# Hybrid retention and RG-LRU layer: five of the eight recurrent input blocks computed by token and turned by DMA, gate matmuls spread one tile a unit

## The chip, the cores and the metric

The kernel runs on one core of one Trainium2 chip. The metric is the time of one execution in device microseconds (us). The kernel before takes 1972.18 us as the median of three runs, which lie between 1972.11 and 1972.3 us.

## The reference, cut to what matters

One decoder layer on 256 tokens of width 2048, everything in float32. The first matrix product, `hn @ w_in`, makes eight slices. Two of them feed the recurrent mixer: `xr` (the recurrent input) and `yr` (its gate).

```python
hn = rmsnorm(h, norm_mix_w[l])
q, k, v, g_ret, xr, yr, g_a, g_b = jnp.split(hn @ w_in[l], offsets, axis=-1)
...                                                     # retention over q, k, v, g_ret -> ret_out
xr = causal_dwconv(xr, rnn_conv_w[l], rnn_conv_b[l])    # 4 taps over the tokens
hr = rg_lru(xr, ...)                                    # 16 blocks of 128 features:
#   gate_r = sigmoid(xb @ w_a + b_a); gate_i = sigmoid(xb @ w_x + b_x)
#   h_t = a_t h_{t-1} + sqrt(1 - a_t^2) (gate_i * xr)_t     a scan over the tokens
rnn_out = jax.nn.gelu(yr) * hr
merged = sigmoid(g_a) * (ret_out @ w_proj_ret[l]) + sigmoid(g_b) * (rnn_out @ w_proj_rnn[l])
h = h + merged @ w_mix_out[l]
...                                                     # cross-attention, conv gated FFN, final norm
```

The convolution and the scan run along the tokens, so the recurrent mixer wants its data with features on the partitions and tokens along the free dimension ("by feature").

## The kernel before

**Products in two parts.** Each float32 matrix is split into a high and a low part (`hi`, `lo` for weights; the two halves of an `s` tile for the activations), and a product is made of three: high by high, activation low by weight high, activation high by weight low. Weights come in pieces of 512 by 512 (1 MB). The work on one piece is a **unit**. A block of 512 output columns of `w_in` takes four units.

**What a unit needs.** `prefetch` issues the DMA of a piece into one of six `raw` buffers on SP's queue, ScalarE (ACT) makes `hi` from it (L288), VectorE (DVE) makes `lo` (L289). Each of `hi` and `lo` has three buffers, and `units` keeps two pieces prepared ahead of the one TensorE (PE) works on. So the cast of a piece can start only when PE has done with the high part of the piece three before it.

**Two ways to multiply.** `gemm_t` leaves its result by feature: the weight is the stationary operand, and the activations move. Per unit it issues 16 matmuls with `hi` that move 512 columns (high and low half of the activations side by side) and 16 with `lo` that move 256 (high half only), and needs two accumulators (`acc`), which are added up afterwards (`joined`: an ACT copy of one half at L552, a DVE addition at L553). `gemm_n` leaves its result by token: the activations are stationary and the weight moves. Per unit it issues 24 matmuls that all move 512 columns, into one accumulator. There are three accumulators in all, of two PSUM banks each.

**Turning by DMA.** A by-token result is turned to by-feature in four steps, which the FFN uses for nearly all of its blocks: `row_planes` splits each float32 word into two 16-bit planes (`rp`), two DMA transposes on SP's queue turn the planes (`d`), `join_planes` puts the words together again (`jp`, four ACT copies a block), and a DVE multiplication by `rsb2` applies the norm's factor of each token.

**The stage that is changed.** `recurrent(b)` for the groups b = 0 to 3 computes two blocks each with `gemm_t`: the recurrent input (`O_XR`, then the convolution into `xr`) and the gate (`O_YR`, then a gelu into `gl`). `recur(b)` follows: `gates(j)` for the four feature tiles (two small matmuls `sm` each at L972, then four ACT functions), then `weigh`, `drive` and `scan`, whose result is stored to DRAM as `rnn`. Group 0 also carries the end of the retention of heads 4 to 7. After the four groups come blocks of `w_in` in pairs.

**What sets the order.** The program is written in units; `later(n, fn)` runs `fn` after n further units. A scheduler then orders each engine's instructions; each engine and each DMA queue runs its own list in order. `tc.keep_in_program_order` holds an instruction at its place in the written order.

Of the kernel before, what the change touches and what calls it, by code (L numbers as in the profile page):

```python
# [14 lines left out]
ALU = mybir.AluOpType  # L15
# [5 lines left out]
NT = D // P  # L21
# [7 lines left out]
BW = 512  # L29
# [12 lines left out]
O_XR, O_YR, O_GA, O_GB = 6144, 8192, 10240, 12288  # L42
# [114 lines left out]
def hybrid_layer(  # L157
# [16 lines left out]
    act, dve, pe, pool, sp = nc.scalar, nc.vector, nc.tensor, nc.gpsimd, nc.sync  # L174
# [17 lines left out]
    def big(shape, dt=F32, s="b"):  # L192
        return bp.tile(shape, dt, tag="big", name=nm(s))
# [112 lines left out]
    def later(n, fn):  # L306

        pending.append((step[0] + n + 1, fn))
# [21 lines left out]
    def gemm_t(w, row, st, nk, col):  # L330

        accs = [acc(), acc()]
        first = gemms[0] == 0
        phase = 0
        for k0, parts in chunks(nk, w, row, col):
            last = k0 + KC >= nk
            tiles = [(kk, j) for j in range(2) for kk in range(KC)]
            if first and k0 == 0:
                runs = [[(t, pr, kk, j) for t in (0, 1)] for pr in range(2) for kk in range(KC) for j in range(2)]
            elif last:  # L340
                runs = [[(t, pr, kk, j) for kk, j in tiles] for pr in range(2) for t in (1 - pr, pr)]
            else:
                runs = [[(t, pr, kk, j) for pr in range(2) for kk, j in tiles] for t in (phase, 1 - phase)]
                phase = 1 - phase
            for i, run in enumerate(runs):
                for t, pr, kk, j in run:
                    k = k0 + kk
                    sx = st[k // 2][:, k % 2, :]
                    part = parts[kk // KH][t][:, kk % KH, (2 * pr + j) * P : (2 * pr + j + 1) * P]
                    a = accs[pr][:, j, :]  # L350
                    if t == 1:
                        a, sx = a[:, S:BW], sx[:, 0:S]
                    pe.matmul(  # L353
                        a, part, sx, start=k == 0 and t == 0, stop=k == nk - 1 and t == 0, skip_group_check=True
                    )
                if i + 1 == len(runs) // 2 and not last:
                    st[(k0 + KC) // 2 + 1]
        return accs
# [14 lines left out]
    def gemm_n(w, row, st, nk, col):  # L373

        a = acc()
        for k0, parts in chunks(nk, w, row, col):
            ops = [
                [halves(st[(k0 + k) // 2], (k0 + k) % 2, slice(tt * P, (tt + 1) * P)) for k in range(KC)]
                for tt in range(2)
            ]  # L380
            for tt in range(2):
                upper_n(a[:, tt, :], ops[tt], parts, k0 == 0)
            for tt in range(2):
                lower_n(a[:, tt, :], ops[tt], parts, k0 + KC >= nk)
        return a
# [272 lines left out]
    xs = Pairs(x_t, p_mix)  # L658
# [21 lines left out]
    rsb2 = rsb[:, None, :].to_broadcast([P, 2, S])  # L680

    def scaled(a, s):
        z = joined(a, s)
        dve.tensor_tensor(out=z, in0=z, in1=rsb2, op=ALU.mult)
        return z
# [72 lines left out]
    def words(t):  # L758

        return t.bitcast(U16).rearrange("p t (w two) -> p t w two", two=2)  # L760

    def planes(t, rows, cs=slice(0, BW)):

        for i in range(2):
            act.copy(t[:, :, i, cs], words(rows)[:, :, :, 1 - i])

    def join_planes(d, pr):

        t = tmp("jp")
        for i in range(2):  # L770
            ins = act.copy(words(t)[:, :, :, 1 - i], d[:, i, 2 * pr : 2 * pr + 2, :])  # L771
            if i == 0:
                tc.keep_in_program_order(ins)
        return t

    def row_planes(o):

        t = big([P, 2, 2, BW], U16, s="rp")
        planes(t, o)
        return t  # L780

    def turn_planes(rows):

        d = big([P, 2, KC, S], U16, s="d")
        for tt in range(2):
            sp.dma_start_transpose(
                out=d.rearrange("p a c s -> p (a c) s")[:, :, tt * P : (tt + 1) * P],
                in_=rows[:, tt].rearrange("p a w -> p (a w)"),
            )
        return d  # L790
# [115 lines left out]
    for g in range(2):  # L906
        dec = big([P, 4, S], s="dec")
        vs, turned = [], []
        for b, o in enumerate((O_Q, O_K)):
            a = qjoin if g == b == 0 else [joined(t, "q") for t in gemm_t("w_in", 0, xs, NT, o + g * BW)]  # L910
# [53 lines left out]
    def recur(b, rgw, xr, gl):  # L964
        aa, tt_, ti = big([P, 4, S], s="aa"), big([P, 4, S], s="tt"), big([P, 4, S], s="ti")

        def gates(j):
            t = 4 * b + j
            c1 = slice(t, t + 1)
            gp = small()  # L970
            for i in range(2):
                pe.matmul(gp[:, i, :], rgw[:, i, j, :], xr[:, j, :], start=True, stop=True)  # L972
            tr = tp.tile([P, S], F32, tag="tr", bufs=2, name=nm("tr"))
            act.activation(tr, gp[:, 0, :], AF.Tanh, scale=0.5, bias=half_ba[:, c1])
            act.activation(ti[:, j, :], gp[:, 1, :], AF.Tanh, scale=0.5, bias=half_bx[:, c1])
            act.activation(aa[:, j, :], tr, AF.Exp, scale=neg_half_c[:, c1], bias=neg_half_c[:, c1])
            act.activation(tt_[:, j, :], tr, AF.Tanh, scale=half_c[:, c1], bias=half_c[:, c1])

        def weigh():
            for pr in range(2):  # L980
                cs = slice(2 * pr, 2 * pr + 2)
                a2 = tmp("a2")
                dve.tensor_tensor(out=a2, in0=aa[:, cs, :], in1=aa[:, cs, :], op=ALU.mult)
                dve.scalar_tensor_tensor(
                    out=tt_[:, cs, :], in0=a2, scalar=1.0, in1=tt_[:, cs, :], op0=ALU.add, op1=ALU.mult
                )
            act.activation(tt_, tt_, AF.Sqrt, scale=0.25)

        def drive():
            dve.scalar_tensor_tensor(out=ti, in0=ti, scalar=1.0, in1=xr, op0=ALU.add, op1=ALU.mult)  # L990
            dve.tensor_tensor(out=ti, in0=ti, in1=tt_, op=ALU.mult)

        def scan():
            for j in range(4):
                dve.tensor_tensor_scan(
                    out=xr[:, j, :], data0=aa[:, j, :], data1=ti[:, j, :], initial=0.0, op0=ALU.mult, op1=ALU.add
                )
            for pr in range(2):
                o = tmp("rn")
                cs = slice(2 * pr, 2 * pr + 2)  # L1000
                dve.tensor_tensor(out=o, in0=xr[:, cs, :], in1=gl[:, cs, :], op=ALU.mult)
                rnn.store(o)

        for j in range(4):
            later(j // 2, lambda j=j: gates(j))
        for n, fn in zip((2, 3, 4) if b < 3 else (6, 11, 17), (weigh, drive, scan)):
            later(n, fn)

    def recurrent(b):
        rgw = big([P, 2, 4, P], s="rgw")  # L1010
        for i, src in enumerate((rg_w_a, rg_w_x)):
            sp.dma_start(out=rgw[:, i], in_=src[0, 4 * b : 4 * b + 4].rearrange("g i j -> i g j"))
        xr = big([P, 4, S], s="xr")
        for pr, a in enumerate(gemm_t("w_in", 0, xs, NT, O_XR + b * BW)):
            z = scaled(a, "xz")
            for j in range(2):
                t = 4 * b + 2 * pr + j
                y = xr[:, 2 * pr + j, :]
                act.activation(y, z[:, j, :], AF.Identity, scale=p_cw(3, t), bias=p_cb(t))
                for s in range(1, 4):  # L1020
                    dve.scalar_tensor_tensor(
                        out=y[:, s:S], in0=z[:, j, 0 : S - s], scalar=p_cw(3 - s, t), in1=y[:, s:S],
                        op0=ALU.mult, op1=ALU.add,
                    )
        gl = big([P, 4, S], s="gl")
        for pr, a in enumerate(gemm_t("w_in", 0, xs, NT, O_YR + b * BW)):
            y = scaled(a, "yz")
            y2, th = tmp("y2"), tmp("yt")
            act.activation(y2, y, AF.Square)
            dve.tensor_scalar(out=y2, in0=y2, scalar1=0.044715 * K0, scalar2=K0, op0=ALU.mult, op1=ALU.add)  # L1030
            dve.tensor_tensor(out=y2, in0=y2, in1=y, op=ALU.mult)
            act.activation(th, y2, AF.Tanh)
            dve.scalar_tensor_tensor(
                out=gl[:, 2 * pr : 2 * pr + 2, :], in0=th, scalar=1.0, in1=y, op0=ALU.add, op1=ALU.mult
            )
        later(0, lambda: recur(b, rgw, xr, gl))

    merged, merged_sums = [], []

# [463 lines left out]
```

## Time and profile before

| | |
|---|---|
| Median of three runs | 1972.18 us |
| The profiled execution, its time | 1972.37 us |
| Its span, first to last instruction | 1970.6 us |
| PE busy | 1959.8 us, 99% of the span |
| DVE, ACT busy | 1563.9 us (79%), 1299.7 us (66%) |
| Mean granted TensorE clock | 0.999 |
| Weight DMAs | 373 of 1 MB, 40 of them on GpSimd's queue |

The page lists busy time per engine, the chain of work that ended last, and groups of instructions by source line. A matmul's listed duration (some 0.39 us) includes its way through the array; matmuls overlap, so the pace is read from the distance between starts. The changed stage lies at about 272 to 482 us of the span.

### The profile page before, as it was taken

To read this page: it belongs to the slowest core of one execution; us is meant where nothing else is said; L and a number is where in the kernel's file an instruction comes from. 1 tells how busy PE (TensorE), PEld (TensorE's weight loads), DVE (VectorE), ACT (ScalarE), POOL (GpSimd) and SP (SyncE) were. 2 spreads that over 40 slices of the span, in tenths; PEclk is the share of its full clock that TensorE was granted. 3 is DMA by queue.
4 is the path that set the end of the run, shared out by engine and by line. 5 is a ranking of instruction groups with operands and counts; after the bars stand their busy time and mean duration, and the time that the engine had idled before them with its cause. 6 is when DMAs were issued, how large, how long until landed. Compare 5 with 4: busy or idle time off the path is not lost.

```text
span 1970.6 us, 23609 instructions
## 1 busy us (share of the span) xinstructions
PE 1959.8 (99%) x9264; PEld 1645.2 (83%) x9264; DVE 1563.9 (79%) x1546; ACT 1299.7 (66%) x1353; POOL 43.2 (2%) x52
## 2 busy tenths in 40 slices
PE   9999999999999999999999999999999999999998
PEld 8888888888888888888888888888888888888887
DVE  6988897889986886778988868777789676796775
ACT  6665656767667656667778767666765577665663
POOL 0000000000000000000000000000000000000000
PEclk9999999999999999999999999999999999999999
DMA  9675774655888876877999749767689677797661
GB/s 370 233 253 149 242 257 171 214 196 157 256 258 244 256 236 213 260 274 232 281 269 230 280 128 248 270 222 212 216 231 315 230 228 229 202 307 270 215 245 64
DMA packets 157598, 461.29 MB, mean 234 GB/s; under 512 B 88368, under 2 KB 93104, under 8 KB 109744
## 3 DMA queue, kind: packets, MB, share of 16 engines
q1 hardware_dynamic: 150208, 415.23, 60.7%
q0 software_dynamic: 5760, 41.95, 11.7%
q10 hardware_dynamic: 1520, 2.63, 0.4%
q8 instruction: 72, 1.18, 0.2%
q14 instruction: 38, 0.31, 0.0%
HBM read 422.01 MB, written 17.83 MB: 223 GB/s over the span
## 4 chain that ended last, share of the span: by engine, by line
PE 96%; DVE 2%; ACT 1%; issue 0%; DMA 0%; SPq 0%; POOLq 0%; ACTq 0%; DVEq 0%
PE acc L371 26%; PE acc L364 26%; PE acc L365 26%; PE acc L353 14%; PE sm L526 2%; PE acc L526 1%; PE sm L972 1%; DVE lo L289 1%; ACT hi L288 0%; PE sm L540 0%; DMA raw<-in_wall 0%; DVE fg L1326 0%; DVE fv L1326 0%; DVE tb L730 0%; DVE raw L296 0%
## 5 line engine op out<-in xcount | busy, mean ns | idle before, releaser
L289 DVE TENSOR_TENSOR lo<-raw,hi 128x2048 fp32r<-128x2048 f32 (+1 forms) x420 | 949.4, 2267 | 271.2 <-ACT hi L288 268.9
L288 ACT CAST hi<-raw 128x2048 fp32r<-128x2048 f32 (+1 forms) x418 | 794.0, 1902 | 483.8 <-PE acc L365 354.0
L364 PE MATMUL acc<-hi,s 128*128 128x512 f32 x2008 | 782.9, 390 | 0.1
L365 PE MATMUL acc<-hi,s 128*128 128x512 f32 x2008 | 781.8, 389 | 0.0
L371 PE MATMUL acc<-lo,s 128*128 128x512 f32 x2008 | 501.0, 389 | 0.0
L371 PEld LDWEIGHTS acc<-lo,s 128*128 128x128 f32 x2008 | 376.9, 188 | 78.3
L364 PEld LDWEIGHTS acc<-hi,s 128*128 128x128 f32 x2008 | 376.9, 188 | 77.8 <-ACT s L563 0.5
L365 PEld LDWEIGHTS acc<-hi,s 128*128 128x128 f32 x2008 | 377.0, 188 | 77.6 <-DVE s L564 0.2
L353 PE MATMUL acc<-s,hi 128*128 128x512 f32 x832 | 201.9, 394 | 0.8 <-DVE hi L286 0.8
L353 PEld LDWEIGHTS acc<-s,hi 128*128 128x128 f32 x832 | 154.2, 189 | 31.7 <-issue 1.1
L771 ACT COPY jp<-d 128x512 uint16<-128x512 uint16 x152 | 108.2, 771 | 36.0 <-DMA d<-rp 34.8
L364 PE MATMUL acc<-hi,ss 128*128 128x512 f32 x320 | 125.3, 392 | 0.6 <-ACT o L462 0.6
L365 PE MATMUL acc<-hi,ss 128*128 128x512 f32 x320 | 124.7, 390 | 0.0
L353 PEld LDWEIGHTS acc<-s,lo 128*128 128x128 f32 x832 | 107.9, 192 | 4.4 <-DVE lo L289 0.7
L353 PE MATMUL acc<-s,lo 128*128 128x256 f32 x832 | 111.0, 284 | 0.2 <-DVE lo L289 0.2
L371 PE MATMUL acc<-lo,ss 128*128 128x512 f32 x320 | 85.6, 389 | 0.0
L364 PEld LDWEIGHTS acc<-hi,ss 128*128 128x128 f32 x320 | 60.1, 188 | 14.1 <-ACT o L462 1.4
L371 PEld LDWEIGHTS acc<-lo,ss 128*128 128x128 f32 x320 | 60.1, 188 | 12.6
L365 PEld LDWEIGHTS acc<-hi,ss 128*128 128x128 f32 x320 | 60.1, 188 | 12.1
L269 POOL DMA_DIRECT2D raw<-in_wall x40 | 35.2, 879 | 1549.4 <-DVE lo L289 976.2
L429 DVE TENSOR_TENSOR nat<-nat,acc 128x512 f32<-128x512 f32 (+1 forms) x45 | 41.3, 930 | 13.9 <-PE acc L371 12.1
L294 DVE TENSOR_TENSOR raw<-raw,raw 128x2048 f32<-128x2048 f32 x20 | 45.8, 2288 | 0.5
(234 smaller groups left out, 1254.9 us busy)
## 6 DMA issues: line engine op xcount, KB each, us to landing
raw<-in_wall SPq DMA_DIRECT2D x333, 1024.0 KB, 5.3
raw<-in_wall POOLq DMA_DIRECT2D x40, 1024.0 KB, 8.2
fkept<-nat SPq DMA_DIRECT2D x12, 512.0 KB, 8.2
nat<-fkept SPq DMA_DIRECT2D x12, 512.0 KB, 4.6
xt<-in_x_t SPq DMA_DIRECT2D x11, 256.0 KB, 7.8
raw<-in_wall SPq DMA_DIRECT2D x5, 512.0 KB, 8.1
nat<-in_x ACTq DMA_DIRECT2D x4, 512.0 KB, 10.0
ret<-hr SPq DMA_DIRECT2D x4, 512.0 KB, 5.5
```

Of the source, the lines that this page charges most:

```text
L269: pool.dma_start(out=raw, in_=src, accum_op=ALU.add)
L288: act.copy(hi[:, a:b], raw[:, a:b])
L289: dve.tensor_tensor(out=lo[:, a:b], in0=raw[:, a:b], in1=hi[:, a:b].bitcast(F32), op=ALU.subtract)
L294: dve.tensor_tensor(out=to, in0=to, in1=by, op=ALU.add)
L353: pe.matmul(a, part, sx, start=k == 0 and t == 0, stop=k == nk - 1 and t == 0, skip_group_check=True)
L364: pe.matmul(o, h, hi, start=start and kk == 0, stop=False, skip_group_check=True)
L365: pe.matmul(o, l, hi, start=False, stop=False, skip_group_check=True)
L371: pe.matmul(o, h, lo, start=False, stop=stop and kk == KC - 1, skip_group_check=True)
L429: dve.tensor_tensor(out=o, in0=o, in1=i, op=op)
L526: ins = pe.matmul(o, a, b, start=start and i == 0, stop=stop and i == 2, skip_group_check=True)
L771: ins = act.copy(words(t)[:, :, :, 1 - i], d[:, i, 2 * pr : 2 * pr + 2, :])
L972: pe.matmul(gp[:, i, :], rgw[:, i, j, :], xr[:, j, :], start=True, stop=True)
```

## The change

The recurrent inputs of groups 0, 1 and 2 and the gates of groups 0 and 1, five blocks of the eight, are computed with `gemm_n` and turned by DMA. Of the two planes of `row_planes`, one is then copied by DVE instead of ACT (`shared`). The turned halves arrive one and two units after the block; convolution and gelu follow there. For groups 0 to 2 the gate tiles are spread over four units, one a unit, instead of two a unit over two, and the steps behind them move from units 2, 3, 4 to 4, 5, 6; `recur` itself starts one unit later for groups 0 and 1. The first gate matmul of each tile is held in the written order. Group 3, and the gate of group 2, stay as they were.

```diff
-    def planes(t, rows, cs=slice(0, BW)):
+    def planes(t, rows, cs=slice(0, BW), shared=False):
         for i in range(2):
-            act.copy(t[:, :, i, cs], words(rows)[:, :, :, 1 - i])
+            copy = dve.tensor_copy if i and shared else act.copy
+            copy(t[:, :, i, cs], words(rows)[:, :, :, 1 - i])
...
             for i in range(2):
-                pe.matmul(gp[:, i, :], rgw[:, i, j, :], xr[:, j, :], start=True, stop=True)
+                ins = pe.matmul(gp[:, i, :], rgw[:, i, j, :], xr[:, j, :], start=True, stop=True)
+                if i == 0:
+                    tc.keep_in_program_order(ins)
...
         for j in range(4):
-            later(j // 2, lambda j=j: gates(j))
-        for n, fn in zip((2, 3, 4) if b < 3 else (6, 11, 17), (weigh, drive, scan)):
+            later(j if b < 3 else j // 2, lambda j=j: gates(j))
+        for n, fn in zip((4, 5, 6) if b < 3 else (6, 11, 17), (weigh, drive, scan)):
             later(n, fn)
...
-        for pr, a in enumerate(gemm_t("w_in", 0, xs, NT, O_XR + b * BW)):
-            z = scaled(a, "xz")
+        def conv_x(pr, z):
...
+        def block(o, by_token, then):
+            if not by_token:
+                for pr, a in enumerate(gemm_t("w_in", 0, xs, NT, o + b * BW)):
+                    then(pr, scaled(a, "xz"))
+                return
+            d = turn_planes(row_planes(gemm_n("w_in", 0, xs, NT, o + b * BW), True))
+            def turned(pr):
+                z = join_planes(d, pr)
+                dve.tensor_tensor(out=z, in0=z, in1=rsb2, op=ALU.mult)
+                then(pr, z)
+            for pr in range(2):
+                later(1 + pr, lambda pr=pr: turned(pr))
+
+        block(O_XR, b < 3, conv_x)
...
+        block(O_YR, b < 2, gelu)
+        later(1 if b < 2 else 0, lambda: recur(b, rgw, xr, gl))
```

On PE, the first unit of group 0's recurrent input. `acc` is an accumulator, `s` an activation tile, `hi` and `lo` the parts of the piece; what stands right behind the arrow is the stationary operand where line 353 is named, and the weight where 364, 365 and 371 are. Before (the first ten rows of the unit):

```order
L353 MATMUL acc_2266<-s_112,hi_2168 128x512 x2
L353 MATMUL acc_2266<-s_123,hi_2168 128x512 x2
L353 MATMUL acc_2266<-s_112,hi_2168 128x512 x2
L353 MATMUL acc_2266<-s_123,hi_2168 128x512 x2
L353 MATMUL acc_2267<-s_112,hi_2168 128x512 x2
L353 MATMUL acc_2267<-s_123,hi_2168 128x512 x2
L353 MATMUL acc_2267<-s_112,hi_2168 128x512 x2
L353 MATMUL acc_2267<-s_123,hi_2168 128x512 x2
L353 MATMUL acc_2266<-s_112,lo_2169 128x256 x2
L353 MATMUL acc_2266<-s_123,lo_2169 128x256 x2
```

The same unit now, from the end of its matmuls with `hi` to the start of the next unit:

```order
L364 MATMUL acc_2266<-hi_2168,s_123 128x512
L365 MATMUL acc_2266<-hi_2168,s_123 128x512
L371 MATMUL acc_2266<-lo_2169,s_112 128x512 x2
L371 MATMUL acc_2266<-lo_2169,s_123 128x512 x2
L371 MATMUL acc_2266<-lo_2169,s_112 128x512 x2
L371 MATMUL acc_2266<-lo_2169,s_123 128x512 x2
L526 MATMUL sm_2297<-s_1421,s_1950 128x256 x3
L526 MATMUL sm_2297<-s_1421,s_1950 128x128 x3
L364 MATMUL acc_2266<-hi_2188,s_137 128x512
L365 MATMUL acc_2266<-hi_2188,s_137 128x512
```

The 16 short matmuls of 256 columns are gone; in their place stand eight of 512, and one accumulator is used instead of two.

On PE again, the start of group 3's recurrent input, which follows the last unit of group 2's gate (both still `gemm_t`). Before, the first piece goes through both new accumulators in turn (`acc_3621` and `acc_3622`, piece `hi_3519`):

```order
L353 MATMUL acc_3621<-s_112,hi_3519 128x512 x2
L353 MATMUL acc_3621<-s_123,hi_3519 128x512 x2
L353 MATMUL acc_3621<-s_112,hi_3519 128x512 x2
L353 MATMUL acc_3621<-s_123,hi_3519 128x512 x2
L353 MATMUL acc_3622<-s_112,hi_3519 128x512 x2
L353 MATMUL acc_3622<-s_123,hi_3519 128x512 x2
```

Now the first accumulator (`acc_3466`) is given all that belongs to it of the first two pieces (`hi_3343`, `hi_3400` and their low parts) and the start of the third before the second accumulator (`acc_3467`) is begun. Ahead of these rows stand eight matmuls with `hi_3343` and four with `lo_3344`:

```order
L353 MATMUL acc_3466<-s_112,lo_3344 128x256 x2
L353 MATMUL acc_3466<-s_123,lo_3344 128x256 x2
L353 MATMUL acc_3466<-s_137,lo_3401 128x256 x2
L353 MATMUL acc_3466<-s_146,lo_3401 128x256 x2
L353 MATMUL acc_3466<-s_137,lo_3401 128x256 x2
L353 MATMUL acc_3466<-s_146,lo_3401 128x256 x2
L353 MATMUL acc_3466<-s_137,hi_3400 128x512 x2
L353 MATMUL acc_3466<-s_146,hi_3400 128x512 x2
L353 MATMUL acc_3466<-s_137,hi_3400 128x512 x2
L353 MATMUL acc_3466<-s_146,hi_3400 128x512 x2
L353 MATMUL acc_3466<-s_160,hi_3470 128x512 x2
L353 MATMUL acc_3467<-s_112,hi_3343 128x512 x2
```

On ACT, the same place: the copies `c` that release group 2's gate accumulators. Before (`acc_3428` is the second of them):

```order
L288 CAST hi_3625<-raw_3623 128x2048
L1029 ACTIVATE y_515_3598<-yz_3594 128x512
L288 CAST hi_3666<-raw_3664 128x2048
L1032 ACT_TABLE_LOAD
L1032 ACTIVATE yt_3599<-y_515_3598 128x512
L552 COPY c_3605<-acc_3428 128x512
```

Now (`acc_3235` is the first of them, `jp` are joins of group 2's turned recurrent input, `d_3231` its turned planes, `tt` the square root of `weigh`):

```order
L772 COPY jp_3329<-d_3231 128x512
L288 CAST hi_3400<-raw_3398 128x2048
L1022 ACTIVATE xr_3055<-jp_3329,pa 128x256 x2
L772 COPY jp_3386<-d_3231 128x512
L288 CAST hi_3470<-raw_3468 128x2048
L990 ACT_TABLE_LOAD
L990 ACTIVATE tt_3139<-tt_3139 128x1024
L772 COPY jp_3386<-d_3231 128x512
L552 COPY c_3438<-acc_3235 128x512
```

The copy that releases `acc_3235` stands behind joins, a cast, a table load and the square root of group 1's chain.

More of the change, by code (lines that the diff above doesn't have):

```diff
@@ L774, in join_planes, with row_planes @@
         return t
-    def row_planes(o):
+    def row_planes(o, shared=False):
         t = big([P, 2, 2, BW], U16, s="rp")
-        planes(t, o)
+        planes(t, o, shared=shared)
         return t
@@ L1024, in recurrent, with gelu @@
                     )
+        def block(o, by_token, then):
[11 more added lines that the diff above has]
+        block(O_XR, b < 3, conv_x)
         gl = big([P, 4, S], s="gl")
-        for pr, a in enumerate(gemm_t("w_in", 0, xs, NT, O_YR + b * BW)):
-            y = scaled(a, "yz")
+        def gelu(pr, y):
             y2, th = tmp("y2"), tmp("yt")
@@ L1035, in recurrent @@
             )
-        later(0, lambda: recur(b, rgw, xr, gl))
+        block(O_YR, b < 2, gelu)
+        later(1 if b < 2 else 0, lambda: recur(b, rgw, xr, gl))
     merged, merged_sums = [], []
```

## Prediction

> **What bounds the kernel now.** I read the page first: the span, the share of each engine, and the chain of work that ended last.
>
> ```profile
> span 1970.6 us, 23609 instructions
> PE 1959.8 (99%) x9264; PEld 1645.2 (83%) x9264; DVE 1563.9 (79%) x1546; ACT 1299.7 (66%) x1353; POOL 43.2 (2%) x52
> PE 96%; DVE 2%; ACT 1%; issue 0%; DMA 0%; SPq 0%; POOLq 0%; ACTq 0%; DVEq 0%
> ```
>
> PE is busy for 1959.8 of 1970.6 us and has 96% of the chain. So time can be saved only by giving PE less to do, and lost only where PE is made to wait. Next I asked for the chain inside the changed stage (285 to 480 us); its columns are start, length and what ran.
>
> ```profile
> by line: PE acc L353 85.7%; PE sm L972 6.2%; PE sm L526 2.9%; PE acc L365 1.9%; PE acc L364 1.9%; PE acc L371 1.5%
> 342.63 1.73 PE sm L972 x8
> 344.36 38.94 PE acc L353 x224
> ```
>
> The whole chain there is PE. Seven units of `gemm_t` follow each other without a gap in 38.94 us, 5.563 us a unit. Last I compared PE's pace in four units of `gemm_t` with that in four of `gemm_n` (a later stage), by windows that begin and end at a start of a unit:
>
> ```profile
> core 0: us, PE busy (x), PEclk, DMA share, GB/s
> 349.75:371.99 22.24, 22.24 (x130) 1.00 0.61 222
> 1296.69:1318.45 21.76, 21.76 (x98) 1.00 0.67 218
> ```
>
> Both run at full granted clock (1.00) with PE always busy: 22.24 us against 21.76.
>
> **The change part by part.** *The matmuls.* Five blocks of four units pass from `gemm_t` to `gemm_n`. By the windows that saves 0.48 us a block, 5 x 0.48 = 2.4 us. The same from the distance between starts, in PE's timeline (x32 is a run of 32 matmuls):
>
> ```profile
> 353.41 4.00 PE L353 MATMUL acc<-s,lo 128*128 128x256 f32 x32
> 357.24 7.44 PE L353 MATMUL acc<-s,hi 128*128 128x512 f32 x32
> 364.52 3.04 PE L353 MATMUL acc<-s,lo 128*128 128x256 f32 x24
> ```
>
> 32 matmuls of 256 columns take 357.24 - 353.41 = 3.83 us (0.120 each), 32 of 512 take 7.28 us (0.2275). A `gemm_t` unit is then 16 x 0.2275 + 16 x 0.120 = 5.56 us, a `gemm_n` unit 24 x 0.2275 = 5.46, a saving of 0.10 us x 20 units = 2.0 us. I take the windows' 2.4, since they hold whole units of both kinds; 2.0 stays as the other end. The Trainium skill (TensorE: Matmul & The Clock Gate, Back-to-back issue gap) speaks against the change: its gap of N/2.4 + 2.5 ns for a lone matmul gives 16 of 512 and 16 of 256 the same time as 24 of 512 within an estimated 0.02 us, so 20 units would save some 0.4 us; the rows above have 120 ns where it has 109, and I go by them.
>
> *The gates.* The 64 matmuls of L972 remain. Spread one tile a unit, they interrupt the stream more often. The chain above shows what an interruption costs: two tiles take 1.73 us for eight matmuls, 0.216 each, with no gap on either side. I cost it at nothing.
>
> *Work added on ACT and DVE.* Neither is on the chain, so the question is whether the casts stay ahead of PE. Busy time over one group (eight units, 336.73 to 384.68 us), and the groups of instructions by line (count | busy, mean ns | idle before):
>
> ```profile
> core 0: us, PE busy (x) PEld busy (x) DVE busy (x) ACT busy (x) POOL busy (x), PEclk, DMA share, GB/s
> 336.73:384.68 47.95, 47.95 (x275) 42.39 (x273) 40.65 (x48) 37.18 (x49) 0.00 (x0) 1.00 0.69 244
> L765 ACT COPY rp<-acc 128x1024 uint16<-128x1024 uint16 x42 | 40.2, 1006 | 0.0
> L771 ACT COPY jp<-d 128x512 uint16<-128x512 uint16 x152 | 108.2, 771 | 36.0 <-DMA d<-rp 34.8
> L552 ACT COPY c<-acc 128x512 f32<-128x512 f32 x26 | 14.9, 580 | 11.3 <-PE acc L353 11.1
> L553 DVE TENSOR_TENSOR xz<-acc,c 128x512 f32<-128x512 f32 x8 | 5.4, 677 | 0.0
> L468 DVE TENSOR_TENSOR o<-o,acc 128x1024 f32<-128x1024 f32 x22 | 26.8, 1217 | 11.0 <-PE acc L371 11.0
> ```
>
> A turned block adds to ACT one plane copy (1.01 us) and four joins (4 x 0.77 = 3.08) and takes away two copies of L552 (2 x 0.58 = 1.16): +2.93 us. With two such blocks ACT goes from 37.18 to 43.0 us of a group of some 47.0. On DVE two additions go (2 x 0.68) and one plane copy out of an accumulator comes. No row shows DVE doing that copy; the nearest are L468, with as many elements and a second operand (1.22 us), and L553, with half as many (0.68). So DVE changes by -0.7 to -0.1 us a block; I take -0.1, the row of equal size. The multiplication by the norm's factor was there before. Both engines still fit beside PE, if PE's weights are ready long before they are used. They are: the tightest cast of this stage in ACT's timeline, and the start in PE's of the run that uses it:
>
> ```profile
> 361.09 1.92 ACT L288 CAST hi<-raw 128x2048 fp32r<-128x2048 f32 x1
> 372.00 1.32 PE L353 MATMUL acc<-s,hi 128*128 128x512 f32 x5
> ```
>
> The cast ends at 363.01, 9.0 us before its use. This lead covers the 2.93 us of one block three times; without it, every microsecond that ACT falls behind would be one of PE's.
>
> *The transposes.* Two for each of five blocks, on SP's queue among the weight pieces. How they go in the stages that have them: the issue's median landing, the landing's min/median/max, the waits of the join (total us, times, longest), and one late case in the timelines of SP and ACT.
>
> ```profile
> d<-rp SPq DMA_TRANSPOSE x60, 3.4
> DMA to landing us min/median/max: 3.1/3.4/7.7
> ACT jp L771 <- DMA d<-rp: 34.8, 20, 4.6
> 1409.89 0.33 SPq L267 DMA_DIRECT2D raw<-in_wall  x1
> 1410.31 5.07 SPq L786 DMA_TRANSPOSE d<-rp  x2
> 1417.51 2.67 ACT L771 COPY jp<-d 128x512 uint16<-128x512 uint16 x4 [0.81 <-DMA d<-rp]
> ```
>
> The first half's join is written one unit (5.5 us) behind the block's end. After the plane copies (1.0 us) and a usual landing (3.4) the data are there at 4.4 us or soon after, so a join waits little. In the late case a weight piece was issued 0.4 us ahead, and the join ran 7.2 us after the transposes' issue. The weight pieces queued behind the transposes have six buffers, and wait behind them in the later stages without PE showing it.
>
> *Steps that come later.* The scan of a group ends two to three units later than before (some 11 to 17 us). Its result is stored and read by these rows (min/median/max ns, first and last start):
>
> ```profile
> L745 SPq DMA_DIRECT2D rnn<-rn x8: 326/327/706, 365.6 to 517.3; - x8
> L752 SPq DMA_DIRECT2D kt<-rnn x8: 319/440/686, 644.0 to 648.5; - x8
> ```
>
> The first read is 126 us behind the last store, which belongs to group 3 and is not moved. Nothing there.
>
> *The place with the least cover* is the start of group 3's recurrent input. Its second accumulator is the one that the gate of group 2 must give back: an ACT copy, then a DVE addition. In the new order PE has 18 matmuls of 512 and 16 of 256 before it needs it, 18 x 0.2275 + 16 x 0.120 = 6.0 us. On ACT stand ahead of the copy (order of the section above) a cast, a table load, a square root and a join; on DVE a low part, `weigh`'s product and a scaling of the turned half.
>
> ```profile
> 350.93 1.28 ACT L987 ACT_TABLE_LOAD   x1
> 352.22 1.06 ACT L987 ACTIVATE tt<-tt 128x1024 f32<-128x1024 f32 x1
> L991 DVE TENSOR_TENSOR ti<-ti,tt 128x1024 f32<-128x1024 f32 x4 | 4.9, 1223 | 0.2
> L684 DVE TENSOR_TENSOR xz<-xz,rsb 128x512 f32<-128x512 f32 x8 | 5.4, 681 | 0.0
> L289 DVE TENSOR_TENSOR lo<-raw,hi 128x2048 fp32r<-128x2048 f32 (+1 forms) x420 | 949.4, 2267 | 271.2 <-ACT hi L288 268.9
> ```
>
> The cast waits for the last eight matmuls with `hi` of the gate, which I estimate to end 1.0 us before the gate does. From the gate's end T then: ACT T - 1.0 + 1.92 + 1.28 + 1.06 + 0.77 + 0.58 = T + 4.6; DVE from the end of the cast T + 0.9 + 2.27 + 1.22 + 0.68 = T + 5.1, and the addition 0.68 more: T + 5.7 to T + 5.8. Against 6.0 us of cover this is a margin of 0.2 to 0.3 us. I take no stall, but it holds only if ACT comes to that cast on time.
>
> *The sum.* The profiled execution took 1972.37 us, 1.8 us outside the span. 1972.37 - 2.4 = 1969.97; the median of the runs, 1972.18, lies 0.19 us lower, which gives 1969.8. I say **1969.9**.
>
> **The rivals.**
>
> *B, the second accumulator is late.* For it: the margin of 0.3 us, against joins that wait up to 4.6 us, and the joins of group 2's turned input stand on ACT ahead of the casts in question. Against it: two units of the gate lie between the joins' place in the program and this one, in which ACT can catch up. If ACT arrives late by 1.3 to 5 us, PE stalls once for as long: 1969.9 + 1.3 to + 5 = 1971.2 to 1974.9; the middle, 1973.0.
>
> *C, slower: ACT's list blocked behind joins.* ACT runs its list in order. A join whose transpose lands as at 1410.31 holds up the cast behind it. The Trainium skill says the same of the engine (TensorE: Matmul & The Clock Gate, Architectural detail: ACT and DVE take their instructions strictly first in, first out), and the kind of wait in the row above agrees. A block costs ACT 2.93 us more; if both of its joins wait 4.6 us, that is 12.1 us, 3.1 beyond the lead of 9.0. It decides from waits that sum to over 6.1 us a block, if nothing is caught up in between. For all five blocks 5 x 3.1 = 15.5 us; for half of them 7.8: 1969.9 + 7.8 = 1977.7 (1975 to 1985). Against it: the median landing, 3.4 us, and 34.8 us of waits in all for 60 transposes, with no row of PE waiting for a join.
>
> *D, the gain is not there.* The `gemm_n` pace was measured in another stage, with other pieces in flight. If the two ways took the same time here, nothing is saved: 1972.2. Against it: full clock and no idle in both windows.
>
> **How the numbers follow.** Forecast 0.63 (1969.3 to 1970.4: up to 0.5 us for the lower price by starts; 0.6 below for unpriced differences between two profiles), B 0.22, C 0.10, D 0.05. A difference of 0.2%, 3.9 us, is about what a measurement of this kernel can tell from no change, so the forecast, nearly all of B, and D count as the same (1968.2 to 1976.1). Slower: C without its mildest end, and B with several stalls, 0.12. Faster would need over 3.9 us, more than the pace of PE can give: 0.03. So 0.85 is left for the same. The range reaches from the forecast's lower end over D and most of B, 1969.3 to 1974.0; it leaves out C and B's upper end.
>
> **What would show it right or wrong.** Right: a turned block's four units last 21.8 us in windows, the granted clock is 1.00, no wait of PE in 272 to 490 us, and the stage ends 2.4 us earlier. B: one idle time of PE, six microseconds into group 3's recurrent input, ended by the DVE addition. C: waits of PE ended by `hi` or `lo` after waits of `jp` for `d`. D: blocks of 22.2 us. Wrong in its base would be a later stage that runs at another pace than before, since nothing is changed there.

## The result, and the profile after

The changed kernel takes 1974.29 us (median of 20 runs, 1972.97 to 1980.08) against 1972.27 us for the kernel before (20 runs, 1971.89 to 1973.91): a ratio of 1.0013, with a 95% interval of 1.0007 to 1.0018. It is 2.0 us slower, where 2.4 us of gain were forecast. That lies within the 0.2% called "the same", but on the other side of zero, and 0.3 us above the range.

The page of the profiled execution (1973.92 us), first the rows that answer to those of before:

```profile
span 1972.1 us, 23312 instructions
PE 1956.5 (99%) x9104; PEld 1636.2 (83%) x9104; DVE 1563.0 (79%) x1541; ACT 1311.0 (66%) x1368; POOL 42.8 (2%) x52
PE 95%; DVE 3%; ACT 1%; issue 0%; DMA 0%; SPq 0%; POOLq 0%; DVEq 0%; ACTq 0%
```

PE is busy for 3.3 us less than before (1956.5 against 1959.8), and yet the span is 1.5 us longer. DVE's share of the chain has grown from 2% to 3%. What PE waited for, longest first (total us, times, longest):

```profile
PE acc L364 <- DVE xz L553: 1.7, 1, 1.7
PE acc L353 <- DVE hi L286: 1.2, 1, 1.2
PE warm L231 <- DVE mhalf L226: 1.1, 1, 1.1
PE acc L353 <- DVE xz L553: 1.0, 1, 1.0
```

The second and third row stand at the kernel's start and were there before (0.8 and 1.1 us). The first and the last are new. Both wait for `xz` of L553, the addition in `joined` that gives an accumulator back. Neither a cast nor a join nor a transpose stands in this list for the stage.

The pace came as forecast. Four units by token in a row, from the third unit of group 1's gate into the third of group 2's input, in a window of PE that begins and ends where the run of `lo` matmuls of a unit starts:

```profile
core 0: us, PE busy (x), PEclk, DMA share, GB/s
362.86:384.62 21.76, 21.76 (x97) 1.00 0.63 197
```

21.76 us, full clock, no idle: the figure of the prediction's second window.

**The first wait** is at the start of group 3's recurrent input, which PE begins at 417.5 us. PE's, ACT's and DVE's timelines, in this order:

```profile
417.52 2.00 PE L353 MATMUL acc<-s,hi 128*128 128x512 f32 x8
...
421.28 2.46 PE L353 MATMUL acc<-s,hi 128*128 128x512 f32 x10
424.78 2.08 PE L353 MATMUL acc<-s,hi 128*128 128x512 f32 x8 [1.05 <-DVE xz L553]
```

```profile
416.77 1.92 ACT L288 CAST hi<-raw 128x2048 fp32r<-128x2048 f32 x1 [1.92 <-PE acc L353]
418.70 1.28 ACT L990 ACT_TABLE_LOAD   x1
420.00 1.06 ACT L990 ACTIVATE tt<-tt 128x1024 f32<-128x1024 f32 x1
420.96 0.77 ACT L772 COPY jp<-d 128x512 uint16<-128x512 uint16 x1
421.59 0.58 ACT L552 COPY c<-acc 128x512 f32<-128x512 f32 x1
```

```profile
415.90 2.45 DVE L1024 SCALAR_TENSOR_TENSOR xr<-jp,pa,xr 128x255 f32<-128x255 f32 x6
418.27 0.69 DVE L987 SCALAR_TENSOR_TENSOR tt<-a,tt 128x512 f32<-128x512 f32 x1
418.87 1.22 DVE L993 SCALAR_TENSOR_TENSOR ti<-ti,xr 128x1024 f32<-128x1024 f32 x1
420.01 2.29 DVE L289 TENSOR_TENSOR lo<-raw,hi 128x2048 fp32r<-128x2048 f32 x1
422.21 1.22 DVE L994 TENSOR_TENSOR ti<-ti,tt 128x1024 f32<-128x1024 f32 x1
423.34 0.69 DVE L1038 TENSOR_TENSOR jp<-jp,rsb 128x512 f32<-128x512 f32 x1
423.94 0.69 DVE L553 TENSOR_TENSOR xz<-acc,c 128x512 f32<-128x512 f32 x1
```

The copy is done at 422.2 us, but the addition behind it starts only at 423.94. DVE was in the convolution, `weigh` and `drive` until 420.0, and began the low part 1.3 us after its cast was done. Before, at the same place, copy and addition were done ahead of PE's first matmul of the block (ACT, DVE and PE, one row each):

```profile
417.39 0.59 ACT L552 COPY c<-acc 128x512 f32<-128x512 f32 x1 [2.76 <-PE acc L353]
418.49 0.68 DVE L553 TENSOR_TENSOR yz<-acc,c 128x512 f32<-128x512 f32 x1
419.95 3.82 PE L353 MATMUL acc<-s,hi 128*128 128x512 f32 x16
```

**The second wait** stands at a place that the prediction doesn't mention: at the first blocks of pairs, behind group 3's gate. ACT, DVE and PE after, and then ACT and DVE at the same place of before:

```profile
466.34 1.91 ACT L288 CAST hi<-raw 128x2048 fp32r<-128x2048 f32 x1 [3.91 <-PE acc L353]
468.15 0.58 ACT L552 COPY c<-acc 128x512 f32<-128x512 f32 x1
468.65 2.29 DVE L289 TENSOR_TENSOR lo<-raw,hi 128x2048 fp32r<-128x2048 f32 x1
470.85 0.69 DVE L553 TENSOR_TENSOR xz<-acc,c 128x512 f32<-128x512 f32 x1
471.69 0.47 PE L364 MATMUL acc<-hi,s 128*128 128x512 f32 x1 [1.69 <-DVE xz L553]
```

```profile
465.34 0.59 ACT L552 COPY c<-acc 128x512 f32<-128x512 f32 x1 [2.76 <-PE acc L353]
466.44 0.68 DVE L553 TENSOR_TENSOR yz<-acc,c 128x512 f32<-128x512 f32 x1
467.15 1.91 ACT L288 CAST hi<-raw 128x2048 fp32r<-128x2048 f32 x1 [1.23 <-DVE yz L553]
```

Before, the copy ran first and the cast behind it. Now ACT idles 3.91 us in front of a cast whose buffer PE still reads, with the copy queued behind that cast, and on DVE the addition queued behind the cast's low part. The lists are in order, so the release is done at 471.5 us, where it was done at 467.1.

### The profile page after: what moved, and what is told of

The parts are those of the page before. It is cut to its first block, busy times and chain, and to the rows that moved or that the text cites. A ratio compares the mean times of both kernels' runs of the same rounds, so it can differ in the third digit from the quotient of the medians.

```text
span 1972.1 us, 23312 instructions
## 1 busy us (share of the span) xinstructions
PE 1956.5 (99%) x9104; PEld 1636.2 (83%) x9104; DVE 1563.0 (79%) x1541; ACT 1311.0 (66%) x1368; POOL 42.8 (2%) x52
## 4 chain that ended last, share of the span: by engine, by line
PE 95%; DVE 3%; ACT 1%; issue 0%; DMA 0%; SPq 0%; POOLq 0%; DVEq 0%; ACTq 0%
PE acc L365 28%; PE acc L364 28%; PE acc L371 28%; PE acc L353 7%; PE sm L526 2%; DVE lo L289 1%; PE acc L526 1%; ACT hi L288 1%; PE sm L973 1%; PE sm L540 0%; DMA raw<-in_wall 0%; DVE xr L1024 0%; DVE tb L730 0%; DVE xz L553 0%; DVE ti L994 0%
## 5 line engine op out<-in xcount | busy, mean ns | idle before, releaser
L364 PE MATMUL acc<-hi,s 128*128 128x512 f32 x2168 | 846.8, 391 | 1.7 <-DVE xz L553 1.7
L365 PE MATMUL acc<-hi,s 128*128 128x512 f32 x2168 | 845.5, 390 | 0.0
L371 PE MATMUL acc<-lo,s 128*128 128x512 f32 x2168 | 540.6, 389 | 0.0
L364 PEld LDWEIGHTS acc<-hi,s 128*128 128x128 f32 x2168 | 407.2, 188 | 85.3 <-issue 2.1
L371 PEld LDWEIGHTS acc<-lo,s 128*128 128x128 f32 x2168 | 407.2, 188 | 84.3
L365 PEld LDWEIGHTS acc<-hi,s 128*128 128x128 f32 x2168 | 407.5, 188 | 83.4
L772 ACT COPY jp<-d 128x512 uint16<-128x512 uint16 x172 | 122.4, 770 | 42.1 <-DMA d<-rp 42.0
L353 PE MATMUL acc<-s,hi 128*128 128x512 f32 x512 | 124.9, 393 | 3.0 <-DVE hi L286 1.2
L353 PEld LDWEIGHTS acc<-s,hi 128*128 128x128 f32 x512 | 94.6, 188 | 22.5 <-issue 3.0
L353 PE MATMUL acc<-s,lo 128*128 128x256 f32 x512 | 69.3, 285 | 0.5 <-DVE lo L289 0.5
L353 PEld LDWEIGHTS acc<-s,lo 128*128 128x128 f32 x512 | 66.5, 191 | 3.8 <-DVE lo L289 1.3
```

What stands on the lines that cost most here:

```text
L353: pe.matmul(a, part, sx, start=k == 0 and t == 0, stop=k == nk - 1 and t == 0, skip_group_check=True)
L364: pe.matmul(o, h, hi, start=start and kk == 0, stop=False, skip_group_check=True)
L365: pe.matmul(o, l, hi, start=False, stop=False, skip_group_check=True)
L371: pe.matmul(o, h, lo, start=False, stop=stop and kk == KC - 1, skip_group_check=True)
```

## The experiments

"Before" is the kernel before on the same chip. "Stage" is the time between two matmuls that all kernels have, one ahead of the stage (234.30 us in before) and one behind it (537.60 us in before, 6,500 matmuls from the end), in the profiled execution, against before's 303.30 us. For the changed kernel these are 234.24 and 539.08 us, 304.84 us, or +1.5. The stage leaves out what differs from one execution to the next at the start of the kernel. It also leaves out a wait of PE near 1910 us, for `s` of L563 in the FFN: 0.4 to 2.3 us in seven of the profiles (1.1 in `turn_only`, 1.9 in `six_early`), none in the two of the changed kernel. Why it comes isn't known. The medians include it.

| kernel | median us (runs) | before us | ratio, 95% interval | stage |
|---|---|---|---|---|
| changed | 1974.29 (20) | 1972.27 | 1.0013, 1.0007 to 1.0018 | +1.5 |
| after_again (the same) | 1973.7 (11) | 1972.5 | 1.0010, 1.0002 to 1.0019 | +1.2 |
| turn_only | 1969.67 (11) | 1972.39 | 0.9989, 0.9980 to 0.9998 | -2.6 |
| spread_only | 1972.42 (11) | 1972.39 | 1.0000, 0.9991 to 1.0009 | +0.1 |
| old_end | 1971.4 (11) | 1972.39 | 0.9997, 0.9988 to 1.0006 | -0.9 |
| two_groups | 1972.73 (11) | 1972.39 | 1.0005, 0.9996 to 1.0013 | -1.2 |
| late_chain | 1976.65 (7) | 1972.25 | 1.0027, 1.0016 to 1.0038 | +4.1 |
| six_turn | 1976.43 (11) | 1972.25 | 1.0023, 1.0014 to 1.0032 | +1.1 |
| eight_turn | 1972.34 (11) | 1972.25 | 1.0000, 0.9992 to 1.0009 | -1.3 |
| eight_blocks | 1973.29 (11) | 1972.25 | 1.0005, 0.9996 to 1.0014 | +0.6 |
| early_release | 1971.81 (11) | 1972.5 | 0.9996, 0.9987 to 1.0004 | -1.3 |
| old_mid | 1972.13 (11) | 1972.5 | 0.9999, 0.9990 to 1.0007 | +0.1 |
| six_early | 1972.54 (12) | 1972.5 | 1.0004, 0.9996 to 1.0013 | -1.4 |
| early_later | 1973.11 (11) | 1972.04 | 1.0006, 0.9997 to 1.0014 | -0.1 |
| six_x | 1970.9 (12) | 1972.04 | 1.0007, 0.9987 to 1.0027 | -3.1 |

### The two halves of the change

`turn_only` keeps the five blocks by token, and takes the moved chain back:

```diff
-            later(j if b < 3 else j // 2, lambda j=j: gates(j))
-        for n, fn in zip((4, 5, 6) if b < 3 else (6, 11, 17), (weigh, drive, scan)):
+            later(j // 2, lambda j=j: gates(j))
+        for n, fn in zip((2, 3, 4) if b < 3 else (6, 11, 17), (weigh, drive, scan)):
```

> The changed kernel with the recurrent chain's old timing: two gate tiles a unit, weighing, drive and scan 2, 3, 4 units behind, nothing held in order; the five blocks by token stay. Three theories. Seams: in the changed kernel PE waited at two places for an accumulator (1.0 us at the start of group 3's input, 1.7 us at the first pair block), because the moved steps of the chain push the copy and the addition that release it behind other work; here the order at the second place is that of before (two casts ahead of the copy, not three), so that stall is gone and the first smaller: 2.2 us of pace less 0 to 1 us, 1970.1 to 1971.2, against 1972.3 before. Joins: the 20 joins and their late transposes hold up ACT wherever the chain's steps stand; then this is no better than the changed kernel, 1973 to 1976, and scatters as widely. Pace: by-token units are no faster here; 1972.3.

It takes 2.7 us less than before, 0.4 us below what was expected, and has the lowest median of all here. Its profile has no wait of PE for an addition, and its order at the start of group 3's input has no square root near the copy. ACT's timeline there:

```profile
411.99 1.40 ACT L772 COPY jp<-d 128x512 uint16<-128x512 uint16 x2
414.88 0.59 ACT L552 COPY c<-acc 128x512 f32<-128x512 f32 x1 [1.49 <-PE acc L353]
```

The copy waits for PE alone, with ACT idle in front of it. All 20 joins are still there, so they aren't what costs. The pace is worth 2.6 us over the stage.

`spread_only` is the kernel before with the moved chain (the lines above the other way round, and the held gate matmul).

> The kernel before with the moved chain alone: gate tiles one a unit, weighing, drive and scan 4, 5, 6 units behind, first gate matmul held in order; no block by token. Seams: the moved steps push releases back even without joins, but with less on ACT; a stall at the start of group 3's input of 0 to 1 us, none at the pair blocks (their order is not that of the changed kernel): 1972.3 to 1973.3. Joins: nothing is turned, so no loss: 1972.3. Interruptions: if the gate matmuls cost more when spread (12 tiles, each with its own break in the stream), 12 x 0.1 = 1.2 us: 1973.5.

No difference. Spread gates cost nothing, as the prediction had it, and the moved chain costs nothing either while nothing is turned. The two halves are worth -2.7 and 0.0 us apart, and together +2.0 (+1.2 on the chip of `after_again`). So the loss comes from the two together.

### Where it arises

`late_chain` is `turn_only` with only the last steps moved (`zip((4, 5, 6) ...`), gates two a unit.

> The five turned blocks with old gates (two tiles a unit, nothing held), but weighing, drive and scan of groups 0 to 2 moved to 4, 5, 6 units as in the changed kernel. The order at the end of group 3's gate is then the changed kernel's: square root and two more casts ahead of the copy, a low part ahead of the addition. Seams by a late chain: a stall of 1.5 to 2.3 us at the first pair block, and 0 to 1.2 us at the start of group 3's input: 1969.7 + 1.5 to 3.5 = 1971.2 to 1973.2. If instead the spread gates or the hold are what costs, this is as the turned blocks alone: 1969.7.

The size was underestimated and the place wrong: PE waits for an addition at the start of group 3's input, and not at the first pair block. PE's waits, its timeline at the wait, and the window right behind it (length, PE busy, granted clock, DMA share, GB/s):

```profile
PE acc L353 <- DVE xz L553: 3.8, 1, 3.8
424.43 3.41 PE L353 MATMUL acc<-s,hi 128*128 128x512 f32 x8 [3.77 <-DVE xz L553]
424.43:427.20 2.77, 2.77 (x7) 0.50 0.39 163
```

The eight matmuls behind the wait take 3.41 us, where eight took 2.08 behind the first wait of the changed kernel; the granted clock there is 0.50. From start to start of PE's matmuls this wait costs 5.3 us, not 3.8. The stage is 6.7 us longer than `turn_only`'s; the other 1.4 us lie in shorter breaks, at a gate matmul (395 us) and in the pair blocks. This execution took 1979.55 us, 2.9 above the median.

So the moved steps are what costs beside the turned blocks; with the gates spread as well, as in the changed kernel, the loss is smaller.

`old_end` has group 2's chain alone at its old times (`(4, 5, 6) if b < 2 else (2, 3, 4)`).

> The changed kernel with only group 2's chain at its old times (gates two a unit, then 2, 3, 4 units). Seams: the scan of group 2 is done before group 3's gate ends, the copy there stands behind two casts as before, and the second stall (1.7 to 2.3 us) is gone; the first stays (group 1's chain still stands there): 1974.3 - 2.0 = 1972.3, and the profile shows PE waiting for an addition once, not twice. Joins: unchanged number of joins, so 1974 to 1975.

As the seams had it, the second wait is gone, and the stage is 2.5 us shorter than the changed kernel's. The first wait, expected to stay as it was, fell to 0.4 us.

`old_mid` has group 1's chain alone at its old times.

> The changed kernel with only group 1's chain at its old times. Seams: group 1's square root and drive no longer stand ahead of the first copy at the start of group 3's input, and the order at the end of group 3's gate has, as a side effect, the copy ahead of the last cast; both stalls under 0.5 us: 1974.3 - 1.2 - 2.3 = 1970.8, at best 1969.9. Joins: 1974.

Only half right. The second wait is gone, but the stage gained just 1.4 us on the changed kernel's: the first wait still has 0.5 us, and there is a new one, in a gate matmul (L973) that waits for ACT to have read the tile before it:

```profile
PE sm L973 <- ACT ti L978: 1.1, 1, 1.1
PE acc L353 <- DVE xz L553: 0.5, 1, 0.5
```

`two_groups` has group 2's input by feature (`block(O_XR, b < 2, conv_x)`).

> The changed kernel with group 2's recurrent input by feature again: four blocks by token, the moved chain as it is. Seams: no join stands ahead of the copies at the start of group 3's input, and the accumulator's copy there comes earlier; the first stall is gone or under 0.5 us, and the order at the pair blocks has the copy behind one cast and the square root, so the second is under 1 us: 4 x 0.43 = 1.7 us of pace less 0 to 1, 1970.6 to 1971.6. Joins: four fifths of the loss stays, 1973.5 to 1974.

The profiled execution was the fastest of its eleven (1971.18 us); the median, 1972.73, is 1 to 2 us above what was expected. In the profile both waits of the changed kernel are gone; PE waits 0.4 us for an addition at another place, inside group 2's gate (399.80 us). Where the other executions (up to 1977.06) lose more stays open.

### A higher rank for the release

`early_release` is the changed kernel with a higher rank for the copy and the addition of `joined` in this stage:

```diff
-        with tc.high_priority(URGENT):
+        with tc.high_priority(60 if s == "xz" else URGENT):
```

> The changed kernel with nothing but the order of the releases touched: the copy and the addition that give an accumulator back have a higher rank for the scheduler. At the end of group 3's gate the copy then stands ahead of the last cast, not behind it, and the addition ahead of that cast's low part; at the start of group 3's input the addition stands ahead of one DVE multiplication. Blocks, joins, transposes and the chain's steps are the same. Seams: the second stall (2.3 us with what follows it) goes, the first (1.2) falls by 0.6: 1974.3 - 2.9 = 1971.4. Joins or late transposes: their number and place are unchanged, so 1974 and the same scatter.

1971.81, by 1.9 us less than the changed kernel on that chip; the stage is shorter by 2.4 to 2.8 us than in its two profiles. ACT and DVE at the first pair blocks:

```profile
466.07 0.59 ACT L552 COPY c<-acc 128x512 f32<-128x512 f32 x1 [2.25 <-PE acc L353]
467.88 1.91 ACT L288 CAST hi<-raw 128x2048 fp32r<-128x2048 f32 x1 [1.22 <-PE acc L353]
469.06 0.68 DVE L553 TENSOR_TENSOR xz<-acc,c 128x512 f32<-128x512 f32 x1
```

The copy stands ahead of the cast again, and PE has no wait there. Blocks, joins, transposes and chain are the same, so the second wait hangs on the order of the lists. The edit is the release's rank alone, but the scheduler also gave other instructions of group 3's blocks new places (casts, steps of the gelu and the gates, a square root). That it is the release's own place, and not theirs, was not tried apart but read from the rows: in the changed kernel the copy and the addition start when the last cast and its low part end; here they run ahead of them. From the first matmul of the pair blocks to the end of the stage it is now 69.69 us, as before and in `turn_only`, against 71.99 in the changed kernel. The first is left with 0.7 us, with DVE's `weigh` and `drive` still ahead of the addition.

`early_later` keeps the higher rank and moves group 1's last steps still later, behind the release (`zip((6, 7, 8) if b == 1 else (4, 5, 6) if b < 3 else ...)`).

> The early release, and group 1's weighing, drive and scan moved still later, to 6, 7, 8 units. Group 1's square root and drive then stand behind the releases at the start of group 3's input and not ahead of them (in the order the copy stands behind two joins, a cast and the convolution's first step). Seams, by what stands ahead of the release: the remaining 0.7 us there is gone although the chain is later than ever; 1971.8 - 0.7 = 1971.1, or less if the chain's work of group 2 falls behind for it. Lateness of the chain as such: worse than the early release, 1973 or more.

The wait at the start of group 3's input is gone, although the chain is later than ever, so lateness as such isn't what costs there. But the total rose, to what lateness as such had forecast (1973 or more). PE now waits for the next two releases: on DVE, group 1's scan, its products and a low part stand ahead of the additions of the first, and group 2's scan and products ahead of the second. PE's timeline, inside group 3's blocks and at the first pair blocks:

```profile
450.76 1.62 PE L353 MATMUL acc<-s,hi 128*128 128x512 f32 x6 [0.52 <-DVE xz L553]
472.75 0.50 PE L364 MATMUL acc<-hi,s 128*128 128x512 f32 x1 [0.99 <-DVE xz L553]
```

### More blocks

`six_turn` is `turn_only` with group 2's gate by token too (`block(O_YR, b < 3, gelu)`), whose chain then starts a unit later (`later(1 if b < 3 else 0, ...)`); `six_early` adds the early release to it.

> The five turned blocks with the old chain, and group 2's gate by token as well (six blocks). Its chain then starts one unit later, and the order at the end of group 3's gate has the square root and a third cast ahead of the copy again, with the scan and a low part ahead of the addition. Seams: 0.47 us more of pace, but the stall at the first pair block is back with 1 to 2 us; no stall at the start of group 3's input, since the block before it needs only one accumulator: 1969.7 - 0.5 + 1 to 2 = 1970.2 to 1971.2. If the place of the chain doesn't matter: 1969.2.

> Six blocks by token with the old chain and the early release. The stall of 2.7 us that six blocks had at the first pair block is gone if the release's place in the order made it (the copy stands behind one cast fewer): 6 x 0.47 = 2.8 us of pace, 1969.4, or up to 1 us more for what six blocks lost elsewhere. If the sixth block's joins were the cause: 1976 as six blocks without it.

The place was right: six blocks wait at the first pair blocks (first row below, `six_turn`), and the early release takes most of that away (second row, `six_early`). The median of `six_turn` is 5 us above the forecast, though, more than its profile (1975.19 us, the fastest of its runs) accounts for, and `six_early` is 3 us above. Of this, 2.0 and 1.6 us lie behind the stage in the two profiles, most of it at the wait near 1910 us. The rest stays open.

```profile
PE acc L364 <- DVE xz L553: 2.9, 2, 2.4
```

```profile
PE acc L364 <- DVE xz L553: 0.7, 1, 0.7
```

`six_x` takes group 3's input as the sixth block instead (`block(O_XR, True, conv_x)`), and leaves group 2's gate and chain alone.

> The five turned blocks with the old chain, and group 3's recurrent input by token as well (six blocks of another choice; group 2's and 3's gates stay by feature). At the end of group 3's gate the copy stands behind a join, a cast and the convolution, no square root and no scan is ahead of it. Seams: stall at the pair blocks 0 to 1 us; 1969.7 - 0.47 + 0 to 1 = 1969.2 to 1970.2. If six blocks are too many for ACT wherever they stand: 1976 as the other six.

The stage is 3.1 us shorter, 0.5 a block, and PE has no wait in it. So it is not the number of blocks. Its median, 1970.9, is no better than `turn_only`'s on another chip; one execution of 1996.14 us makes its interval wide, and its profile has the wait near 1910 us, with 1.7 us.

`eight_turn` and `eight_blocks` turn all eight blocks (both calls of `block` with `True`, and `later(1, ...)`), with the old and with the moved chain.

> All eight blocks by token, old chain. No block that needs two accumulators is left in the stage, so by the theory of the seams PE waits for no addition there: 8 x 0.47 = 3.8 us of pace, 1968.5. Joins: 32 joins in place of 20, and those of group 3's gate fall among the pair blocks, where the casts are only 0.9 to 4.8 us ahead of PE; if ACT is the limit there, PE waits for casts by 2 to 6 us: 1970.5 to 1974.5.

> All eight blocks by token with the moved chain of the changed kernel. Seams: no accumulator to wait for, so the moved chain costs nothing here, and this equals the eight blocks with the old chain within 0.5 us, near 1968.5. If the moved chain costs by itself (casts held up behind it), it stays 4 us above the old chain's run.

With no pair of accumulators left in the stage, no wait for an addition is in either profile, as the seams had it. But the gain is eaten in the pair blocks. In `eight_turn` a gate matmul of group 3 waits for ACT to have read an earlier tile,

```profile
PE sm L973 <- ACT ti L976: 2.5, 1, 2.5
```

and in `eight_blocks` PE waits 1.8 us for a copy of a pair block (`o`, L462). That the joins of group 3's gate are what keeps ACT busy there was not tried apart. The moved chain makes 1.0 us of difference here by the medians and 1.9 in the profiles' stages, where 0.5 was forecast at most. The executions of the two overlap, so whether the chain costs something where no such release is left stays open.

### The changed kernel again

> The changed kernel once more, unaltered, for a second profile and its scatter on this chip: 1974.3 (1973 to 1980). Seams: the added time of a slow execution stands at the same two places, as longer waits for the addition. Late transposes: it stands at casts behind joins in groups 1 and 2.

The profiled execution (1974.66 us) has the same two waits for the addition, 0.7 and 1.7 us. At 1974.66 us it is near the middle of its runs, so what the longest ones (1979.41 us) wait for stays open.

## Why the prediction was wrong

- **Pace**: right. 2.4 us were forecast, 2.6 measured (`turn_only`'s stage), and 3.1 for six blocks. The windows were the better choice than the distances between starts (2.0). The Trainium skill's gap for a lone matmul (TensorE: Matmul & The Clock Gate, Back-to-back issue gap), which gave 0.4 us, is not borne out.
- **Gates**: right, 0.0 us (`spread_only`).
- **ACT's and DVE's added work**: right. DVE's plane copy took 1.22 us (the value taken), and PE never waited for a cast in the stage. Rival C did not happen in any profile; joins of the stage waited up to 3.4 us in the changed kernel, and the lead covered it.
- **Steps that come later: the step that failed first.** "Nothing there" looked only at who reads the scan's result, 126 us later. The steps themselves are work on ACT and DVE, and moving them by two or three units put them in front of other work in two lists that run in order. What a moved step now stands ahead of was asked at one place only, and there in part (the next two points).
- **The place with the least cover**: the place and the mechanism of rival B, and the wrong size. ACT's half was right (T + 4.6, and the copy was done at 422.2 against T = 417.5). DVE's half let the low part begin as soon as the cast was done, T + 0.9; it began at T + 2.5, behind the convolution, a step of `weigh` and the first of `drive`, which the sum had left out (the product that it calls `weigh`'s is `drive`'s second). The addition ended at T + 7.1 and not T + 5.7, and the margin of 0.3 us became a wait of 1.0.
- **One place where there were two.** The same release stands at every end of a `gemm_t` block. The order of the lists at the end of group 3's gate had changed too, and the prediction doesn't read it. That second wait was the larger (1.7 us, with what followed it 2.3 in the stage). The stage is 4.1 us longer than `turn_only`'s: 1.3 us of this at the first wait, from start to start of PE's matmuls, 2.3 at the second, and some 0.5 in breaks too short for the view.

Rival B's range (to 1974.9) held the result, but the stated range stopped at 1974.0. That B held it is in part luck: the one wait that B names was 1.05 us, under its lower end of 1.3, and the larger one was at a place that B doesn't have.

## What to carry to other kernels

When a change moves a step in time, price it twice: by who needs its result, and by what it now stands ahead of on its engine. Look first at the short instructions that give a buffer back to the bounding engine; here they cost nothing until longer work, part of it waiting for that same engine, was put ahead of them. And a change that gains by pace and loses by order can be cut in two: here the gain was in one half alone, and the kernel with that half is faster than both.

## What the runs showed of the hardware

The transposes of the stage took longer to land than the usual ones: 5.1 us in the median of ten, against 3.4 us in the median of the 60 of the kernel before, which all stand behind the stage. The longest of the ten took 6.6 us, the longest of the 60 took 7.7. The transposes of the changed kernel and ACT's waits for them, both over 272 to 482 us:

```profile
L787 SPq DMA_TRANSPOSE d<-rp x10: 1232/1358/3034, 301.5 to 402.4; - x10
DMA to landing us min/median/max: 4.0/5.1/6.6
ACT jp L772 <- DMA d<-rp: 9.1, 4, 3.4
```

The Trainium skill (Advanced Engine Details and Errata, X-Bar Transpose) calls them as fast as regular DMAs. The time to landing doesn't bear this out here: the store `rnn<-rn`, of as many bytes as one of the transposes (256 KB), landed in 2.9 us before (median of eight). The transposes are issued in pairs on one queue, though, and their rate was not measured. PE waited for none of them.

A wait of PE can cost more than its length. Behind the one of 3.77 us in `late_chain` the granted clock was 0.50 over 2.8 us, and behind one of 2.26 us in `old_end` (1911 us) 0.51 over 3.5 us; behind waits of 2.40 us in `six_turn` and 2.50 us in `eight_turn` it was 1.00. What decides between the two is not worked out here.
